# Recurrent branch of a hybrid step: another form of the decay root, gate products on VectorE, weights split one stage earlier and kept in DRAM

## The chip, the core and the metric

The kernel runs on one core of a Trainium2 chip. The metric is the device time in microseconds (us) of one launch. The engines of the core run side by side, each its own instructions in their written order: TensorE (PE, matrix products), VectorE (DVE), ScalarE (ACT), GpSimd (POOL) and SyncE (SP, which here issues most of the DMA transfers). An instruction starts when those ahead of it on its engine have started and the semaphores it waits for are set, so an instruction that waits holds up all that is written behind it on its engine.

## The reference, cut to what matters

One step of a two-layer backbone on 512 latent tokens and 128 context tokens, width 1024. The even layer has two branches, attention and a gated linear recurrence (RG-LRU) over 512 channels in both directions, and one output projection over both. The odd layer is differential attention. What the change touches is the recurrence:

```python
def rglru(x, w_a, b_a, w_x, b_x, lam, h0, reverse):
    ...
    r = jax.nn.sigmoid(jnp.einsum('btnc,ncd->btnd', xb, w_a).reshape(b, t, wd) + b_a)
    i = jax.nn.sigmoid(jnp.einsum('btnc,ncd->btnd', xb, w_x).reshape(b, t, wd) + b_x)
    log_a = -LRU_C * r * jax.nn.softplus(-lam)
    a = jnp.exp(log_a)
    u = jnp.sqrt(-jnp.expm1(2 * log_a)) * (i * x)
    ...
    a_acc, u_acc = lax.associative_scan(combine, (a, u), reverse=reverse, axis=1)
    hs = u_acc + a_acc * h0[:, None, :]
    final = hs[:, 0] if reverse else hs[:, -1]
    return hs, final

def even_layer_lat(...):
    ...
    o_a = neighbourhood_attention(q, k, v, ck, cv, rpb).reshape(b, t, NA_WIDTH)
    o_b, _, _ = lru_branch(xb, conv_w, conv_b, wa, ba, wx, bx, lam, lru_state[:, 0], lru_state[:, 1])
    o = jnp.concatenate([o_a * jax.nn.silu(ga), o_b * jax.nn.silu(gb)], axis=-1) @ w_out
    return x + gate * o
```

The combine step is h[t] = a[t]·h[t-1] + u[t]. `lru_branch` runs a depthwise convolution of width 4 and then `rglru` in both directions, and adds the two.

Products are done in three matmuls of a split operand (hi·hi + lo·hi + hi·lo), so every weight and every activation that goes into TensorE is first split into a rounded part `hi` and the rest `lo`.

## The kernel before, in words

One program runs in five stages, in each of which TensorE's work is a list of matmul groups (`fill`) and all the rest are `side` tasks. `run` merges the two: each group of the list has a cost, and a side task is written into the program when the sum of the costs reaches the task's position. The positions and lags stand in tables of numbers at the top of the file (`E1_POS`, `LRU_POS`, `LRU_LAG`, `XB_LAG`, `E3_POS` and so on). So the order of the instructions on each engine is fixed when the program is built.

The stages, with their times in the profiled execution:
- E0, to 75 us: conditioning and the V projection.
- E1, 75 to 218.5 us, the attention stage: 8 neighbourhood-attention heads, with the q, k and gate projections between them.
- E2, 218.5 to 330.4 us, the recurrent stage: the projections xb (input of the recurrence) and gb (its gate), the recurrence in 4 blocks of 128 channels (numbers 0 to 3 in the names, so xc3 is block 3), and the half "oa" of the output projection (attention part, `opea` in the names).
- E3, 330.4 to 386.6 us: the other half "eb" of the output projection (recurrent part, `op`), the residual, the norm of the odd layer (transposes `trx`), V of the odd layer.
- O, to 787.7 us: differential attention and the final norm.

A block of the recurrence: `xb_fill` copies the projection into `XB` (ACT), makes the convolution `xc` (one ACT and three DVE instructions, L791 to L793) and splits it into `xh` and `xl`. `lru_gate` makes the four gate products `g` on PE, with tanh on ACT into `thr` (decay gate) and `thi` (input gate), L814. `lru_a` makes `aa` = a (exp, L824) and tanh(L825) on ACT, (1+thi)·xc on DVE (L826), a² into `ss` on POOL (L828) and thr = (ss+1)·thr on DVE (L829), which is 1-a². `lru_b`, once for two blocks, takes the root on ACT (L835) and multiplies thi by it (L839: 6 of the 8 products on POOL, 2 on DVE). `lru_c` runs the four scans of a block on DVE (L846 to L853), copies the final states (`fin`) and adds both directions on POOL (L856). `lru_d` multiplies the sum into the gate path `oT` on DVE (L862, L864). `thr` and `thi` have two buffers each, so the first gate of block 2 waits until `lru_d` of block 0 has read its buffer.

Weights: a class keeps a list of loads. SP loads one of 512 KB into a staging tile (`_st`), ACT makes `hi` (L101), DVE makes `lo` by a subtraction (L102). The output weights of the even layer are four such loads for "oa" (`woea00` to `woea11`) and four for "eb" (`woeb00` to `woeb11`); the gate weights of the recurrence are four loads `lws` of 256 KB, split in E2 too.

## Time and profile before

| | us |
|---|---|
| median of 3 runs (790.59 to 790.83) | 790.82 |
| the profiled execution, its own time | 789.51 |
| its span, first to last instruction | 787.7 |
| PE busy, of the span | 738.8 (94%) |
| DVE busy | 566.7 (72%) |
| ACT busy | 401.0 (51%) |
| POOL busy | 276.9 (35%) |

The rows of the trace stand further down in numbered groups. Times in them are microseconds from the start of the span unless marked ns. In a timeline row the first number is the start, the second the duration, then engine, source line, operation, output and inputs, shape, and in brackets how long the engine stood idle before it and what released it. A row of waits gives the total, the count and the longest. A row of instructions by line gives the count and the durations in ns as minimum/median/maximum, or busy time and mean. Granted clock (PEclk) is TensorE's clock as a share of the full 2.4 GHz; its lower level is 1.2 GHz.

### The profile page before, as it was taken

The page shows a single profiled execution, that of the slowest core. Times are in us where ns is not written, and L with a number is a line of the kernel's source. Part 1 is how long each engine was busy: PE and PEld are TensorE (multiplying, and loading weights), DVE is VectorE, ACT ScalarE, POOL GpSimd, SP SyncE. Part 2 cuts the span into 40 slices and gives each one's busy share as a digit, 9 for nine tenths or more (in the row PEclk, how much of TensorE's full clock was granted, in tenths as well). Part 3 has the DMA queues.
Part 4 walks back from the last instruction along what each step waited for, and adds up shares of the span by engine and source line. Part 5 has one row for each costly group of instructions (what it writes and reads, how often), then busy time and mean ns, then how long its engine had stood idle before and what let it go on. Part 6 is the DMA issues. An engine that isn't in the chain of part 4 may idle for free.

```text
span 787.7 us, 13005 instructions
## 1 busy us (share of the span) xinstructions
PE 738.8 (94%) x4964; PEld 674.5 (86%) x4964; DVE 566.7 (72%) x1009; ACT 401.0 (51%) x836; POOL 276.9 (35%) x257
## 2 busy tenths in 40 slices
PE   4999999999999878799989999999999999999993
PEld 2679999989889866577989999999999999978872
DVE  3446677776656989868566678676878687887966
ACT  5355456555547675147444545545555555553423
POOL 3221211121001746443474164425544363212354
PEclk9999999999999989899999999999999999999997
DMA  8825433432381124395241122022211312241203
GB/s 343 319 72 188 171 112 114 141 125 101 111 303 65 51 84 134 109 378 188 96 146 47 64 88 74 22 89 66 68 44 47 117 55 78 64 139 49 91 1 133
DMA packets 33630, 92.32 MB, mean 117 GB/s; under 512 B 4272, under 2 KB 9200, under 8 KB 33568
## 3 DMA queue, kind: packets, MB, share of 16 engines
q1 hardware_dynamic: 31248, 88.10, 32.0%
q10 hardware_dynamic: 1920, 3.15, 1.7%
q8 instruction: 39, 0.64, 0.3%
q0 software_dynamic: 400, 0.25, 0.1%
q14 instruction: 23, 0.19, 0.1%
HBM read 79.94 MB, written 8.39 MB: 112 GB/s over the span
## 4 chain that ended last, share of the span: by engine, by line
PE 41%; DVE 9%; ACT 3%; issue 1%; POOL 1%; DMA 0%; ACTq 0%; DVEq 0%; POOLq 0%
PE ov L183 2%; PE ov L184 2%; PE ov L185 2%; PE dk L183 2%; PE dk L185 2%; PE dk L184 2%; PE opoa L185 2%; PE ds L1204 2%; PE opoa L183 2%; PE ds L1203 2%; PE dpt L1242 2%; PE opoa L184 2%; PE dq L183 2%; PE dq L185 2%; PE dq L184 2%; PE dg L183 1%
## 5 line engine op out<-in xcount | busy, mean ns | idle before, releaser
L1208 ACT ACTIVATE de<-ds,dnm 128x640 f32<-128x640 f32 x64 | 51.0, 796 | 105.6 <-DVE dnm L1206 105.6
L1206 DVE TENSOR_REDUCE dnm<-ds 128x1 f32<-128x640 f32 x64 | 52.3, 818 | 22.7 <-PE ds L1299 10.6
L569 POOL TENSOR_SCALAR_AFFINE_SELECT Tm<-rb 128x64 f32<-128x64 f32 (+1 forms) x24 | 8.8, 366 | 112.0 <-DMA rb<-in_rpb 93.2
L183 PE MATMUL ov<-owv_hi,hT_hi 128*128 128x256 f32 x160 | 46.5, 291 | 0.1
L184 PE MATMUL ov<-owv_lo,hT_hi 128*128 128x256 f32 x160 | 45.3, 283 | 0.0
L185 PE MATMUL ov<-owv_hi,hT_lo 128*128 128x256 f32 x160 | 45.2, 282 | 0.0
L183 PE MATMUL dk<-hT_hi,dk_hi 128*128 128x320 f32 x128 | 41.7, 326 | 0.0
L183 PE MATMUL dq<-hT_hi,dq_hi 128*128 128x320 f32 x128 | 41.0, 320 | 0.5 <-ACT vc L1092 0.5
L183 PE MATMUL dg<-hT_hi,dg_hi 128*128 128x320 f32 x128 | 41.0, 320 | 0.0
L1204 PE MATMUL ds<-dKL,dQ 128*128 128x320 f32 x128 | 38.9, 312 | 1.9 <-DVE dKL L487 1.9
L185 PE MATMUL dk<-hT_hi,dk_lo 128*128 128x320 f32 x128 | 40.3, 314 | 0.0
L184 PE MATMUL dk<-hT_lo,dk_hi 128*128 128x320 f32 x128 | 40.2, 314 | 0.0
L185 PE MATMUL dq<-hT_hi,dq_lo 128*128 128x320 f32 x128 | 39.6, 309 | 0.0
L185 PE MATMUL dg<-hT_hi,dg_lo 128*128 128x320 f32 x128 | 39.6, 309 | 0.0
L184 PE MATMUL dq<-hT_lo,dq_hi 128*128 128x320 f32 x128 | 39.6, 309 | 0.0
L184 PE MATMUL dg<-hT_lo,dg_hi 128*128 128x320 f32 x128 | 39.6, 309 | 0.0
L1203 PE MATMUL ds<-dKH,dQ 128*128 128x320 f32 x128 | 39.4, 316 | 0.1
L1230 DVE SCALAR_TENSOR_TENSOR de<-de,drs,de 128x640 f32<-128x640 f32 x32 | 35.8, 1120 | 1.1
L102 DVE TENSOR_TENSOR PTl<-pt,PTh 128x512 fp32r<-128x512 f32 x24 | 16.6, 692 | 26.0 <-ACT PTh L101 24.4
L102 POOL TENSOR_TENSOR dq_lo<-dq_st,dq_hi 128x1024 fp32r<-128x1024 f32 x8 | 21.4, 2678 | 29.9 <-ACT dq_hi L101 29.9
L183 PEld LDWEIGHTS ov<-owv_hi,hT_hi 128*128 128x128 f32 x160 | 30.3, 190 | 1.0 <-DVE sgdg L468 0.5
L102 DVE TENSOR_TENSOR dPTl<-dpt,dPTh 128x512 fp32r<-128x512 f32 (+1 forms) x48 | 28.5, 594 | 3.7 <-ACT dPTh L101 3.7
(481 smaller groups left out, 2788.2 us busy)
## 6 DMA issues: line engine op xcount, KB each, us to landing
aste<-in_e_ada_w SPq DMA_DIRECT2D x16, 512.0 KB, 5.7
asto<-in_o_ada_w SPq DMA_DIRECT2D x16, 512.0 KB, 5.5
astge<-in_e_ada_g SPq DMA_DIRECT2D x8, 512.0 KB, 6.1
owv_st<-in_o_wv SPq DMA_DIRECT2D x8, 512.0 KB, 3.3
astgo<-in_o_ada_g SPq DMA_DIRECT2D x8, 512.0 KB, 7.1
dq_st<-in_o_w SPq DMA_DIRECT2D x8, 512.0 KB, 3.3
dk_st<-in_o_w SPq DMA_DIRECT2D x8, 512.0 KB, 3.5
dg_st<-in_o_w SPq DMA_DIRECT2D x8, 512.0 KB, 3.3
```

What stands on the lines that cost most here:

```text
L102: after(lag, lambda: (eng.tensor_tensor(lo, src, hi.bitcast(F32), ALU.subtract), done and done()))
L183: PE.matmul(out, ah, bh, start=start, stop=False)
L184: PE.matmul(out, ah, bl, start=False, stop=False)
L185: PE.matmul(out, al, bh, start=False, stop=stop)
L569: G.affine_select(dst, src, pattern=[[8, n], [0, 8]], compare_op=ALU.is_ge, fill=NEG, base=8 * jj + 7, channel_multiplier=-1)
L1203: PE.matmul(sp[:, b, 0:HALF], qs, KH[:, a, ks], start=True, stop=False)
L1204: PE.matmul(sp[:, b, 0:HALF], qs, KL[:, a, ks], start=False, stop=True)
L1206: V.tensor_reduce(nm[:, a : a + 1], sp[:, :, 0:HALF], AX.XY, ALU.max, negate=True)
L1208: S.activation(e, sp[:, :, 0:HALF], AF.Exp, bias=nm[:, a : a + 1], accum_out=rs[:, a : a + 1])
L1230: V.scalar_tensor_tensor(e0_, e0_, rs[:, 0:1], e1_, ALU.mult, ALU.add)
L1242: PE.transpose(tp[:, 256 * m + 128 * c : 256 * m + 128 * c + 128], p[:, 128 * kt : 128 * kt + 128], ident)
```

## The change

- The root. sqrt(1-a²) is made as (1+a)·sqrt(tanh(...)), with half the argument in the tanh. The square on POOL is gone, and so is its tile. The root is taken of `thr` straight after the tanh, and one DVE instruction for each block, thr = (aa+1)·thr, stands behind the root instead of ahead of it.
- All 8 gate products are on DVE. The sum of both directions stays on POOL for blocks 0 to 2 and is on DVE for block 3; it goes into `thi`.
- `thr` and `thi` have three buffers.
- Ten splits are made in E1: for each, SP loads 512 KB into `est`, ACT casts `hi` into a part of `oT` that is not used yet, DVE subtracts in place, and SP stores both parts to DRAM. Two carry the gate weights, eight the output weights. In E2 and E3 their `hi` and `lo` come from DRAM by two loads in place of one, with no work on ACT or DVE.
- The tables of positions for E2, E3 and the early splits have other numbers. The O stage's step is the same 13.0 under another name.

The core of the diff:

```diff
-            lambda: V.tensor_scalar_mul(cn, u3, 4.0),
+            lambda: V.tensor_scalar_mul(cn, u3, 2.0),
...
-            woea.append([W.add(I["e_wo"][i, q], [128, 2, 512], f"woea{i}{q}") for q in range(2)])
+            woea.append([W.late(f"woea{i}{q}", [128, 2, 512]) for q in range(2)])
...
+                if src is None:
+                    need(("early", name))
+                    for dst, x in zip((hi, lo), self.parts[name]):
+                        SP.dma_start(dst[:].bitcast(F32), x)
+                    put("w", self.done)
...
+    ehis = [oT[:, k : k + 2].rearrange("p a b -> p (a b)")[:, 0:1024].bitcast(F32R) for k in (4, 6)]
+    def early_split(n, p):
...
+        def load():
+            st["w"] = ep.tile([128, 1024], F32, tag="est", name=f"est{n}", bufs=EARLY_BUFS)
+            SP.dma_start(st["w"], src if len(shape) == 4 else src.rearrange("p a b -> p (a b)"))
+        def low():
+            V.tensor_tensor(st["w"][:].bitcast(F32R), st["w"], ehi.bitcast(F32), ALU.subtract)
+        def store():
+            put("early", name)
+            SP.dma_start(flat[0], ehi.bitcast(F32))
+            SP.dma_start(flat[1], st["w"])
+        return [(p - EARLY_LAG[0], load), (p, lambda: S.copy(ehi, st["w"])), (p + EARLY_LAG[1], low), (p + EARLY_LAG[2], store)]
...
-            st["thr"] = lp.tile([128, 2, XL], F32, tag="thr", name=f"thr{i}", bufs=2)
-            st["thi"] = lp.tile([128, 2, XL], F32, tag="thi", name=f"thi{i}", bufs=2)
+            st["thr"] = lp.tile([128, 2, XL], F32, tag="thr", name=f"thr{i}", bufs=3)
+            st["thi"] = lp.tile([128, 2, XL], F32, tag="thi", name=f"thi{i}", bufs=3)
...
-        for d in range(2):
-            G.tensor_tensor(ss[:, d], aa[:, d], aa[:, d], ALU.mult)
-        after(LRU_LAG[0], lambda: (V.scalar_tensor_tensor(thr, ss, 1.0, thr, ALU.add, ALU.mult), put("la", i)))
+        put("la", i)
...
-            thr, thi = lru_st[j]["thr"], lru_st[j]["thi"]
+            thr, thi, aa = lru_st[j]["thr"], lru_st[j]["thi"], lru_st[j]["aa"]
+            V.scalar_tensor_tensor(thr, aa, 1.0, thr, ALU.add, ALU.mult)
             for d in range(2):
-                (V if ((1, 0), (0, 0), (1, 0), (0, 0))[j][d] else G).tensor_tensor(thi[:, d], thi[:, d], thr[:, d], ALU.mult)
+                (G if LRU_POOL[j][d] else V).tensor_tensor(thi[:, d], thi[:, d], thr[:, d], ALU.mult)
...
-        G.tensor_tensor(hs[:, 0], hs[:, 0], hs[:, 1], ALU.add)
+        (G if LRU_POOL[i][2] else V).tensor_tensor(u[:, 0], hs[:, 0], hs[:, 1], ALU.add)
...
-    hooks = {(0, 0): lambda: W.split(wob[1][0], E3_LAG[3]), (0, 2): lambda: W.split(wob[1][1], E3_LAG[4]),
+    hooks = {(0, 2): lambda: W.split(wob[1][1], E3_LAG[4]),
```

How the instructions stand now, at three places. First VectorE in the recurrent stage, around the convolution of the fourth block, xc3 (the last number in a name only tells tiles apart). Before, from the second gate of the third block on:

```order
L468 SCALAR_TENSOR_TENSOR oT_127<-sgtgb21_3267,gb2_1_3233 128x320
L839 TENSOR_TENSOR thi0_2994<-thi0_2994,thr0_2993 128x644
L846 SCALAR_TENSOR_TENSOR thr0_2993<-aa0_3076,lru_s_269,thi0_2994 128x512
L847 SCALAR_TENSOR_TENSOR thr0_2993<-aa0_3076,thi0_2994 128x128
L852 SCALAR_TENSOR_TENSOR thr0_2993<-aa0_3076,lru_s_269,thi0_2994 128x512
L853 SCALAR_TENSOR_TENSOR thr0_2993<-aa0_3076,thi0_2994 128x128
L102 TENSOR_TENSOR woea00_lo_3313<-woea00_st_3105,woea00_hi_3312 128x1024
L793 SCALAR_TENSOR_TENSOR xc3_3346<-XB1_2830,conv_265,xc3_3346 128x644 x3
L862 SCALAR_TENSOR_TENSOR oT_127<-thr0_2993,oT_127 128x8x64
L864 SCALAR_TENSOR_TENSOR oT_127<-thr0_2993,oT_127 128x128
```

And now, from the same gate on:

```order
L489 SCALAR_TENSOR_TENSOR oT_127<-sgtgb21_3333,gb2_1_3297 128x320
L846 SCALAR_TENSOR_TENSOR xc3_3393<-XB1_2910,conv_265,xc3_3393 128x644 x3
L891 SCALAR_TENSOR_TENSOR thr0_3107<-aa0_3301,thr0_3107 128x1288
L893 TENSOR_TENSOR thi0_3108<-thi0_3108,thr0_3107 128x644 x2
L891 SCALAR_TENSOR_TENSOR thr1_3196<-aa1_3272,thr1_3196 128x1288
L893 TENSOR_TENSOR thi1_3197<-thi1_3197,thr1_3196 128x644 x2
L107 TENSOR_TENSOR xl3_3399<-xc3_3393,xh3_3398 128x644
L489 SCALAR_TENSOR_TENSOR oT_127<-sgtgb30_3435,gb3_0_3400 128x320
L900 SCALAR_TENSOR_TENSOR thr0_3107<-aa0_3301,lru_s_269,thi0_3108 128x512
L901 SCALAR_TENSOR_TENSOR thr0_3107<-aa0_3301,thi0_3108 128x128
```

The convolution xc3 stood behind the scans of block 0 and a weight split and stands ahead of them now; the roots and products of blocks 0 and 1 stand between it and its split xl3.

Second, SyncE's queue at the end of the recurrent stage, from the last "oa" weight to the first loads of E3 (`xae` and `spill` are the residual's tiles and their way to DRAM, `xr` is the residual's load in E3). Before:

```order
L120 DMA woea11_st_3427<-in_e_wo 128x1024
L962 DMA xaexa_3464<-in_xs 128x512 x2
L962 DMA xaegbias_3465<-in_xp 128x512
L120 DMA woeb00_st_3501<-in_e_wo 128x1024
L969 DMA spill2_67<-xaexa_3464 128x512 x2
L969 DMA spill2_67<-xaegbias_3465 128x512
L962 DMA xaegbias_3465<-in_xs 128x512
L962 DMA xaexa_3464<-in_xs 128x512
L120 DMA woeb01_st_3631<-in_e_wo 128x1024
L962 DMA xaexa_3464<-in_xp 128x512
L120 DMA woeb10_st_3658<-in_e_wo 128x1024
```

Now:

```order
L149 DMA woea11_hi_3669<-woea11_h_703 128x1024
L149 DMA woea11_lo_3670<-woea11_l_704 128x1024
L1023 DMA spill2_67<-xaegbias_3512 128x512
L1016 DMA xaexa_3511<-in_xp 128x512
L149 DMA woeb00_hi_3696<-woeb00_h_705 128x1024
L149 DMA woeb00_lo_3697<-woeb00_l_706 128x1024
L1023 DMA spill2_67<-xaegbias_3512 128x512
L1023 DMA spill2_67<-xaexa_3511 128x512
L149 DMA woeb01_hi_3779<-woeb01_h_707 128x1024
L149 DMA woeb01_lo_3780<-woeb01_l_708 128x1024
L1023 DMA spill2_67<-xaexa_3511 128x512
L1057 DMA out_lru<-fin_118 128x8
```

Each output weight is two loads straight into the tiles that TensorE reads, and woea11 now stands behind seven of the residual's transfers that it stood ahead of (they are above this piece). The load of woeb10 follows behind out_lru, the store of the final states.

Third, VectorE in the attention stage, in the third of its four parts. Before:

```order
L606 RECIPROCAL rs23_1537<-rs23_1537 128x1
L607 TENSOR_SCALAR P23_1535<-P23_1535,rs23_1537 128x384
L508 TENSOR_REDUCE cnme1_1565<-cs10_1563 128x1
L508 TENSOR_REDUCE cnme1_1565<-cs11_1564 128x1
L300 TENSOR_SCALAR MTo_108<-adaTo2_1577,o_ada_bT_259 128x2
L301 TENSOR_SCALAR MTo_108<-adaTo2_1577,o_ada_bT_259,o_normT_261 128x2
L102 TENSOR_TENSOR PTl20_1591<-pt20_1585,PTh20_1590 128x512
```

Now:

```order
L627 RECIPROCAL rs23_1577<-rs23_1577 128x1
L628 TENSOR_SCALAR P23_1575<-P23_1575,rs23_1577 128x384
L770 TENSOR_TENSOR est3_1387<-est3_1387,oT_127 128x1024
L529 TENSOR_REDUCE cnme1_1611<-cs10_1609 128x1
L529 TENSOR_REDUCE cnme1_1611<-cs11_1610 128x1
L321 TENSOR_SCALAR MTo_108<-adaTo2_1623,o_ada_bT_259 128x2
L322 TENSOR_SCALAR MTo_108<-adaTo2_1623,o_ada_bT_259,o_normT_261 128x2
L107 TENSOR_TENSOR PTl20_1637<-pt20_1631,PTh20_1636 128x512
```

The subtraction of the fourth early split (est3) is a new row ahead of the softmax work of the next heads; the other nine stand in the same way at other places of the stage.

## Rows read from the trace of the kernel before

**Rows 1.** Windows by stage: E1, then E2; the first line names the columns.
```profile
core 0: us, PE busy (x) PEld busy (x) DVE busy (x) ACT busy (x) POOL busy (x), PEclk, DMA share, GB/s
75.00:218.50 143.50, 142.96 (x1102) 132.85 (x1101) 97.67 (x264) 77.67 (x186) 19.85 (x65) 1.00 0.37 127
218.50:330.40 111.90, 95.77 (x546) 84.11 (x544) 92.61 (x95) 65.36 (x88) 49.15 (x33) 0.95 0.35 121
```
**Rows 2.** Waits of PE, whole run: total us, times, longest.
```profile
PE g L183 <- ACT thr L814: 7.1, 1, 7.1
...
PE op L183 <- ACT oh L101: 2.4, 1, 2.4
PE op L185 <- DVE ol L102: 2.2, 1, 2.2
...
PE opea L184 <- DVE woea_lo L102: 1.9, 1, 1.9
...
PE opea L183 <- ACT woea_hi L101: 1.6, 1, 1.6
PE trx L1066 <- DVE xo L1056: 1.2, 1, 1.2
```
**Rows 3.** Timeline of PE: the matmuls that end its longest and its last E2 wait.
```profile
280.42 0.64 PE L183 MATMUL g<-xh,lwh 128*128 128x322 f32 x1 [7.10 <-ACT thr L814]
...
330.42 0.80 PE L185 MATMUL op<-woeb_hi,ol 128*128 128x512 f32 x1 [2.22 <-DVE ol L102]
```
**Rows 4.** Timeline of ACT in the same stretch as the long wait.
```profile
277.01 0.73 ACT L101 CAST xh<-xc 128x644 fp32r<-128x644 f32 x1 [8.64 <-DVE xc L793]
278.27 1.28 ACT L814 ACT_TABLE_LOAD   x1 [0.53 <-DVE oT L864]
```
**Rows 5.** Timeline of DVE, ops with and without POOL beside them.
```profile
252.47 2.74 DVE L793 SCALAR_TENSOR_TENSOR xc<-XB,conv,xc 128x644 f32<-128x644 f32 x3 [1.52 <-ACT xc L791]
...
260.53 1.50 DVE L829 SCALAR_TENSOR_TENSOR thr<-ss,thr 128x1288 f32<-128x1288 f32 x1
...
265.14 2.49 DVE L846 TENSOR_TENSOR_SCAN thr<-aa,lru_s,thi 128x512 f32<-128x512 f32 x1
...
273.09 3.89 DVE L793 SCALAR_TENSOR_TENSOR xc<-XB,conv,xc 128x644 f32<-128x644 f32 x3
276.89 1.08 DVE L862 SCALAR_TENSOR_TENSOR oT<-thr,oT 128x512 f32<-128x512 f32 x1
...
278.09 1.28 DVE L846 TENSOR_TENSOR_SCAN thr<-aa,lru_s,thi 128x512 f32<-128x512 f32 x1
...
281.09 0.81 DVE L102 TENSOR_TENSOR xl<-xc,xh 128x644 fp32r<-128x644 f32 x1
```
**Rows 6.** Instructions of three lines, E2: ns minimum/median/maximum, first and last start.
```profile
L826 DVE SCALAR_TENSOR_TENSOR thi<-thi,xc x8: 821/1356/1891, 243.2 to 300.6; 128x644 f32<-128x644 f32 x8
L828 POOL TENSOR_TENSOR ss<-aa x8: 1678/1827/1845, 243.4 to 301.9; 128x644 f32<-128x644 f32 x8
L856 POOL TENSOR_TENSOR thr<-thr x4: 1556/1582/2197, 273.2 to 323.0; 128x644 f32<-128x644 f32 x4
```
**Rows 7.** DVE by line and shape, 218 to 331: busy us, mean ns, idle before.
```profile
L102 DVE TENSOR_TENSOR woea_lo<-woea_st,woea_hi 128x1024 fp32r<-128x1024 f32 x4 | 7.1, 1774 | 0.7 <-ACT woea_hi L101 0.7
...
L102 DVE TENSOR_TENSOR woeb_lo<-woeb_st,woeb_hi 128x1024 fp32r<-128x1024 f32 x3 | 3.6, 1211 | 0.0
...
L102 DVE TENSOR_TENSOR lwl<-lws,lwh 128x512 fp32r<-128x512 f32 x4 | 2.7, 686 | 1.3 <-ACT lwh L101 1.3
```
**Rows 8.** ACT by line and shape in E1: a cast of 1024 columns.
```profile
L101 ACT CAST k_hi<-k_st 128x1024 fp32r<-128x1024 f32 x3 | 3.2, 1052 | 0.0
```
**Rows 9.** Waits of DVE in E1: total us, times, longest.
```profile
DVE PTl L102 <- ACT PTh L101: 24.4, 23, 2.0
```
**Rows 10.** DMA issues 215 to 345: count, KB each, median us to landing.
```profile
woea_st<-in_e_wo SPq DMA_DIRECT2D x4, 512.0 KB, 3.5
```
**Rows 11.** Windows of 10 us: the start of E3.
```profile
330.00:340.00 10.00, 9.58 (x31) 7.70 (x32) 4.62 (x6) 1.05 (x1) 2.68 (x2) 0.72 0.89 288
```

More of the change, by code (lines that the diff above doesn't have):

```diff
@@ L34 @@
 LAG_E1 = (2.13, 0.0)
-LAG_E2 = (0.2, 3.75)
-LAG_E3 = (3.85, 1.06)
+LAG_E2 = (0.0, 4.36)
+LAG_E3 = (4.55, 1.39)
 LAG_O = (1.0, 0.98)
@@ L62 @@
 HOLD = 2
+EARLY_LAG = (8.46, 0.92, 1.0)
+EARLY_POS = ((5.4, 8.46, 16.0), (3.43, 13.56, 16.4), (3.0, 14.38, 12.44), (2.99,))
+EARLY_BUFS = 2
+LRU_POOL = ((0, 0, 1), (0, 0, 1), (0, 0, 1), (0, 0, 0))
 KORD = (0, 2, 4, 6, 1, 3, 5, 7)
@@ L114, in add, with late @@
             return len(self.todo) - 1
+        def late(self, name, shape, pool=None, bufs=None):
+            return self.add(None, shape, name, pool, bufs)
         def load(self, n):
@@ L133, in split @@
                     lo = pool.tile(list(shape), F32R, tag="wlo", name=name + "_lo", bufs=bufs)
+                if src is None:
+                    need(("early", name))
+                    for dst, x in zip((hi, lo), self.parts[name]):
+                        SP.dma_start(dst[:].bitcast(F32), x)
+                    put("w", self.done)
+                    self.ready[self.done] = (hi, lo)
+                    self.done += 1
+                    self.load(self.done + 1)
+                    continue
                 st = self.staged.pop(self.done)
@@ L408, in body @@
         if kind == "oa":
-            woa.append([W.add(I["e_wo"][i, q], [128, 2, 512], f"woea{i}{q}") for q in range(2)])
+            woa.append([W.late(f"woea{i}{q}", [128, 2, 512]) for q in range(2)])
         else:
             wid[f"{kind}{i}"] = wcol("e_w", (12 if kind == "xb" else 16) + i, f"{kind}{i}")
-    wob = [[W.add(I["e_wo"][half, 2 + q], [128, 2, 512], f"woeb{half}{q}", *(("op", 2) if half else ())) for q in range(2)] for half in range(2)]
+    wob = [[W.late(f"woeb{half}{q}", [128, 2, 512], *(("op", 2) if half else ())) for q in range(2)] for half in range(2)]
     W.hold = wob[1][0]
@@ L729, in gb_fill @@
         return proj_silu(ep if i < 2 else lp, wid[f"gb{i}"], f"gb{i}", lambda sg: None, oT[:, 4 + i])
+    early = [(I["lru_w"][2 * n : 2 * n + 2].rearrange("i p g n -> p i g n"), [128, 2, 4, 128], f"lw{n}") for n in range(2)]
+    early += [(I["e_wo"][i, 2 * x + q], [128, 2, 512], f"woe{'ab'[x]}{i}{q}") for x in range(2) for i in range(2) for q in range(2)]
+    ehis = [oT[:, k : k + 2].rearrange("p a b -> p (a b)")[:, 0:1024].bitcast(F32R) for k in (4, 6)]
+    def early_split(n, p):
+        src, shape, name = early[n]
+        ehi = ehis[n % 2]
+        W.parts[name] = [dram.tile(shape, F32, tag=f"{name}_{x}", name=f"{name}_{x}") for x in "hl"]
+        flat = [p.rearrange("p a b c -> p (a b c)" if len(shape) == 4 else "p a b -> p (a b)") for p in W.parts[name]]
+        st = {}
+        def load():
[8 more added lines that the diff above has]
+        return [(p - EARLY_LAG[0], load), (p, lambda: S.copy(ehi, st["w"])), (p + EARLY_LAG[1], low), (p + EARLY_LAG[2], store)]
     fill = q_fill(0) + k_fill(0)
@@ L734, in body @@
     now = sum(c for c, _ in fill)
+    n_early = 0
     for i in range(4):
@@ L747, in body @@
         side += na_ctx(i, start + E1_POS[i][2])
+        for p in EARLY_POS[i]:
+            side += early_split(n_early, start + p)
+            n_early += 1
         if i < 3:
@@ L773, in lru_w @@
     def lru_w(i):
-        st = lp.tile([128, 4, 128], F32, tag="lws", name=f"lws{i}")
-        SP.dma_start(st, I["lru_w"][i])
+        need(("early", f"lw{i // 2}"))
         hi = lp.tile([128, 4, 128], F32R, tag="lwh", name=f"lwh{i}", bufs=2)
@@ L778, in lru_w @@
         lw[i] = (hi, lo)
-        return lambda: (split(hi[:], lo[:], st[:]), put("lw", i))
+        for dst, x in zip((hi, lo), W.parts[f"lw{i // 2}"]):
+            SP.dma_start(dst[:].bitcast(F32), x[:, i % 2])
+        put("lw", i)
     def xb_fill(i):
@@ L815, in lru_gate @@
                      bias=lb[:, 4 * i + g : 4 * i + g + 1])
+        put("g", i)
     def lru_a(i):
+        need(("g", i), n=4)
         st = lru_st[i]
@@ L820, in lru_a @@
         st["aa"] = aa = lp.tile([128, 2, XL], F32, tag="aa", name=f"aa{i}", bufs=2)
-        st["ss"] = ss = lp.tile([128, 2, XL], F32, tag="ss", name=f"ss{i}")
         for d in range(2):
@@ L1023, in body @@
     W.pools["op"], W.hold = op, None
+    W.split(wob[1][0])
     wvo = {0: [W.add(I["o_wv"][0, q], [128, 4, 256], f"owv0{q}") for q in range(2)]}
```

30 lines of the change are left out of this document (16 added, 14 removed).

## The prediction
> **What bounds the kernel now.** I read the windows by stage first [rows 1]. In E1 TensorE is busy 142.96 of 143.50 us: nothing there can be won, it can only be lost. In E2 it is busy 95.77 of 111.90, and VectorE 92.61, more than any other helper. So E2 is the stage to look at, and 111.90 - 95.77 = 16.1 us of idle PE are what an edit in it can give back. The granted clock of 0.95 means that a tenth of the time ran at the lower level, about 0.05 x 111.9 = 5.6 us lost; PE's own work in E2 is therefore 95.77 - 5.6 = 90.2 us, and PE alone could be done with E2 at 218.5 + 90.2 = 308.7. No gain from E2 can be over 21.7 us.
>
> Next the waits of PE over the whole run [rows 2]. One takes 7.1 us, the first gate of block 2; then come four of 1.6 to 2.4 on splits of output weights and of the recurrent output. I followed the long one back. The gate matmul needs its `xh` and a free `thr`. `xh` starts at 277.01 after 8.64 us in which ACT waited for xc [rows 4], so ACT was ready at 268.37. xc started on DVE only at 273.09 and took 3.89 [rows 5], because scans of block 0 and a weight split stood ahead of it. The tanh then waits for `lru_d` of block 0, the last reader of the buffer [rows 4]. The matmul restarts at 280.42 [rows 3]. The last wait of E2 ends at 330.42 [rows 3], on `ol`, the end of a DVE chain of scans, lru_d and splits. Behind it the first 10 us of E3 have clock 0.72 [rows 11]. So E2 is bound by the in-order DVE, first at xc3, then at ol.
>
> **The price of POOL beside DVE.** The same DVE instruction is longer when a POOL instruction on SBUF runs beside it: L826 takes 821 ns at least and 1891 at most [rows 6], a scan 1.28 or 2.49, the convolution 2.74 or 3.89 [rows 5]. That is +1.07, +1.21, +1.15; I take 1.1 us for each overlap.
>
> **Removed.** From DVE in E2 and the first rows of E3: four woea_lo (7.1), three woeb_lo (3.6), four lwl (2.7), in sum 13.4 us [rows 7], inflation of two woea_lo included. From ACT about as many casts; ACT has room, so they count for nothing by themselves, but two waits of PE (woea_hi 1.6, woea_lo 1.9) [rows 2] lose their cause. From POOL: eight squares of 1.83 and six products. Their overlaps with DVE go with them.
>
> **Added to DVE.** Six of the eight products at 0.82 (L826's undisturbed 821, same width): +4.9. The root instruction, 1.5 as L829 undisturbed [rows 5], takes the place of L829, so 0. One sum of directions: +0.8. Net on DVE in E2: 13.4 - 5.7 = 7.7 less, before contention.
>
> **Moved: the walk along DVE.** Nothing ahead of xc3 sits in PE's way, before or now, so PE comes to xb3 at the same time and ACT hands over xc at 268.37 as above. By the order, DVE has nothing but two splits and the pair for block 0 ahead of that and is free: xc3 starts at 268.4 instead of 273.09. From there I add what stands on DVE up to the first ol: xc3 2.74; four roots of 1.5; eight products, four thi, one sum and xl3, 14 of 0.82; four scan sets at 3.0 (278.09 to 281.09 [rows 5]); four lru_d at 1.2 (276.89 to 278.09); 5 splits of ooa, 6 gated products, 2 residual sums, one ol, 14 of 0.69 (512 columns, as lwl); two gate products of some 0.5. Sum 2.7 + 6.0 + 11.5 + 12.0 + 4.8 + 9.7 + 1.0 = 47.7. Rows that follow each other overlap a little (273.09 + 3.89 = 276.98 against a next start of 276.89 [rows 5]); with 0.05 for each of some 30 that I did not take start to start it is 1.5: 46.2. Start 268.4 + 46.2 = 314.6. Six POOL instructions still run beside it (sums of directions for blocks 0 to 2, three or so residual sums): + 6 x 1.1 = 6.6. Waits that I see left (the sum of block 2 on POOL, the cast of oh): 1.3. The first ol is then ready, and E3 in full course, at 322.5 instead of 330.42: **7.9 us gained.** Since DVE is never free on this way, PE's shorter waits don't add to it. They are: first gate of block 2 some 2.2 us, still behind two table loads, two roots and a cast on ACT (three buffers spare it the lru_d); ooa some 3.7, now behind roots, products and scans; woea11 1.1, its loads wait for the tile's last reader (3.0 us of matmuls against 3.5 from issue to landing [rows 10]); end of E2 4.8, much as now.
>
> **Early splits in E1.** Ten times a cast of 1.05 on ACT [rows 8] and a subtraction of 1.21 on DVE [rows 7] go into in-order queues beside a PE that never waits. In this stage DVE waits 24.4 us in 23 times for the probabilities' cast [rows 9], about 1.06 each, so there is idle time near most of the splits. The bound below is 0. The bound above is the whole 22.6 us on PE's way, if each stands in a chain that PE waits for; the trace shows idle ahead of the consumers, so I take 0.7 (one split of ten in full view of a wait with little slack, a third of 2.27) and keep 0 to 4.
>
> **E3.** The loads of woeb10 and woeb11 stand on SP behind out_lru, which waits for POOL's last final states, and hi and lo are 1 MB in a stretch where DMA engines are 0.89 busy [rows 11]: 0 to 2 us. The transposes come some 0.5 earlier in the fill, so their present wait of 1.2 [rows 2] grows by about 0.7. I take 1.0 together, range 0 to 3. O is the same: 0.
>
> **Sum.** 7.9 - 0.7 - 1.0 = 6.2. The profiled execution of 789.51 becomes 783.3; the median of 790.82, 1.3 above it, becomes **784.6**.
>
> **The rivals.**
> B, contention nearly gone. If the remaining POOL instructions fall into places where DVE reads PSUM or waits, the walk ends at 316 to 318.8, the gain is 11.6 to 14 with part of the low clock avoided, and after 0.7 to 1.7 of cost the time is 777 to 780. For it: POOL had 49.15 us in E2 [rows 1] and loses over half. Against: the six left lie just on the part where DVE is never idle.
>
> C, DVE stands still for the whole of each POOL instruction, and loads come late. A convolution started within 0.1 us of a POOL sum that took 2.20 (median 1.58 [rows 6]) and lost 1.15 [rows 5], so the trace shows less than a whole stop. If it were whole, six overlaps would cost up to 1.58 each, 9.5 in place of 6.6, E3 would start at 325.4, and 5.0 less 1.7 for E1 and E3 leaves 787.5; with woea11 and woeb11 up to 1 us late each, up to 789.5.
> By the Trainium skill, SBUF — State Buffer, section "SBUF: two separate sides", the port that VectorE and GpSimd share is a lock held for a whole instruction, and the loser blocks. The sum by that rule alone would be 787.5 where mine is 784.6, and the trace agrees with it only in part, with its 1.15 of 1.58.
>
> S, no difference: E2 ends on a latency chain from cast to subtraction to sum that the moved work doesn't shorten, and the early splits eat the rest: 789.3 to 792.3. For it: the end-of-E2 wait is about as long by my walk as now.
>
> D, slower: the early splits stand in chains. Each adds 1.05 on ACT and 1.21 on DVE, 2.26 in series for whatever is written behind it, the cast and the split of the probabilities above all, where the idle time is some 1.06 each [rows 9]. If PE's chain has no more slack than that, a split costs 2.26 - 1.06 = 1.2; with two of the ten away from the probabilities that is 9.6, and 7.9 - 9.6 - 1.0 = -2.7 gives 793.5. It decides from 0.7 us per split, where the gain is gone. For it: PE busy without a gap says only that work comes in time, not with how much to spare. Against it: DVE is busy 97.67 of 143.50 and ACT 77.67 [rows 1], so what a split delays can catch up before the next one, some 14 us later.
>
> **How the numbers follow.** A .52, B .16, C .14, S .10, D .08. The likeliest is A: 784.6, its own range 782 to 787. For 8 in 10 I leave out the lower part of B (.08), D (.08) and what of S is above 790 (.05): 779 to 790. About 0.2%, 1.6 us, is what a measurement of this kernel can tell from no change. Faster by more than that: A, B and C, .82; within it, S, .10; slower, D, .08.
>
> **What would show it right or wrong.** Right: xc3 starts on DVE near 268.4, PE's wait for the first gate of block 2 falls from 7.1 to some 2, DVE runs without a gap from there to ol, the POOL instructions beside it cost about 1.1 each, the first ol ends near 322, E1 ends within 1 us of 218.5. Wrong in E1: new waits of PE on DVE or ACT there, and each later stage late by as much. Wrong in the walk: gaps on DVE ahead of a scan or a root, which would mean that ACT's roots and table loads, not DVE, set the pace. Wrong in E3: PE waiting for woeb10 or woeb11 from DMA.

## The result

The changed kernel takes 782.17 us (median of 4 runs, 780.81 to 783.55) against 790.71 of the kernel before beside it: ratio 0.9901, interval 0.9884 to 0.9918. The forecast was 784.6. Beside some of the experiments it was measured once more with 782.77 against 790.62, ratio 0.9898. The profiled execution took 782.90 by its own time (span 781.1), 6.6 less than the 789.51 of before. The medians differ by 8.5, since before's profile lies 1.2 below the 790.71 and this one 0.7 above its median; so the traces account for 6.6 of the 8.5.

To see where, I cut the PE timeline of every kernel at the same matmuls: E1 from the first V projection to the first xb, E2 from there to the third group of the "eb" half, E3a to the eighth of its second item, E3b until the odd layer's key projections are under way, O1 through the odd layer's first scores, and the rest. All are differences of start times of one profiled execution.

| kernel | time ratio to before | E1 | E2 | E3a | O1 |
|---|---|---|---|---|---|
| before | 1 | 199.6 | 114.5 | 17.7 | 71.3 |
| changed | 0.9901 | 200.5 | 109.5 | 17.7 | 69.7 |
| changed, again | 0.9898 | 199.9 | 109.1 | 18.7 | 69.8 |

The two stretches left out (E3b with 18.9 us up to V and 26.1 or 25.3 behind it; the rest of O with 308.8 to 309.1) differ by 0.8 and 0.3. So E2 gained 5.0, E3b 0.8 and O1 1.6, and E1 lost 0.9; another 0.4 was lost ahead of E1.

The windows by stage of the changed kernel, with the columns of [rows 1]:

```profile
75.00:219.50 144.50, 143.60 (x1101) 132.72 (x1100) 110.21 (x276) 85.67 (x195) 26.07 (x64) 1.00 0.70 235
219.50:326.00 106.50, 95.59 (x547) 83.59 (x546) 74.58 (x91) 56.59 (x77) 19.99 (x18) 0.97 0.46 164
```

VectorE's busy time in E2 fell from 92.61 to 74.58 and GpSimd's from 49.15 to 19.99; PE's idle time there only from 16.1 to 10.9. The waits of PE from the first xb on, which answer [rows 2]:

```profile
PE op L204 <- ACT oh L106: 3.5, 1, 3.5
PE opea L206 <- DVE ooa L107: 2.3, 1, 2.3
PE g L204 <- ACT thr L867: 1.9, 1, 1.9
PE trx L1121 <- DVE xo L1111: 1.8, 1, 1.8
PE opea L204 <- DMA woea_hi<-woea_h: 1.3, 1, 1.3
PE opea L204 <- ACT ooa L106: 1.0, 1, 1.0
PE opea L205 <- DMA woea_lo<-woea_l: 0.8, 1, 0.8
```

The wait of 7.1 for the first gate of block 2 is 1.9 now, the two on weight splits (1.9 and 1.6) are gone, and of the two at the end of E2 (2.4 and 2.2) one of 3.5 is left. Two new kinds stand in their place: for ooa on VectorE (that on ACT, 1.0, was there before), and for the DMA of woea11. The timeline of VectorE, at the places that answer [rows 5]:

```profile
269.81 2.74 DVE L846 SCALAR_TENSOR_TENSOR xc<-XB,conv,xc 128x644 f32<-128x644 f32 x3 [2.04 <-ACT xc L844]
272.46 1.50 DVE L891 SCALAR_TENSOR_TENSOR thr<-aa,thr 128x1288 f32<-128x1288 f32 x1
...
283.01 3.15 DVE L107 TENSOR_TENSOR ooa<-oT,ooa 128x512 fp32r<-128x512 f32 x3
...
290.87 2.58 DVE L880 SCALAR_TENSOR_TENSOR thi<-thi,xc 128x644 f32<-128x644 f32 x2
...
295.90 0.69 DVE L953 TENSOR_TENSOR optmpae<-opea,gate_e 128x512 f32<-128x512 f32 x1 [0.60 <-PE opea L206]
...
302.86 2.55 DVE L893 TENSOR_TENSOR thi<-thi,thr 128x644 f32<-128x644 f32 x2
...
310.19 0.69 DVE L953 TENSOR_TENSOR optmpae<-opea,gate_e 128x512 f32<-128x512 f32 x1 [1.76 <-PE opea L206]
...
316.87 0.69 DVE L953 TENSOR_TENSOR optmpae<-opea,gate_e 128x512 f32<-128x512 f32 x1 [1.68 <-PE opea L206]
...
319.10 2.31 DVE L900 TENSOR_TENSOR_SCAN thr<-aa,lru_s,thi 128x512 f32<-128x512 f32 x1
...
325.94 1.29 DVE L107 TENSOR_TENSOR ol<-oT,oh 128x512 fp32r<-128x512 f32 x2 [0.54 <-ACT oh L106]
```

The convolution xc3 starts as soon as ACT hands it over and has its undisturbed 2.74 instead of 3.89. The first ol starts at 325.94. On the way there are four rows lengthened by GpSimd (3.15, 2.58, 2.55, 2.31) and, unlike the forecast, three that wait for PE (0.60, 1.76, 1.68).

### The profile page after: what moved, and what is told of

The parts are those of the page before. It is cut to its first block, busy times and chain, and to the rows that moved or that the text cites. A ratio compares the mean times of both kernels' runs of the same rounds, so it can differ in the third digit from the quotient of the medians.

```text
span 781.1 us, 13085 instructions
## 1 busy us (share of the span) xinstructions
PE 735.6 (94%) x4964; PEld 670.1 (86%) x4964; DVE 559.7 (72%) x1014; ACT 399.4 (51%) x834; POOL 252.9 (32%) x242
## 3 DMA queue, kind: packets, MB, share of 16 engines
q10 hardware_dynamic: 1920, 3.15, 1.6%
## 4 chain that ended last, share of the span: by engine, by line
PE 39%; DVE 10%; ACT 3%; issue 1%; POOL 1%; DMA 0%; ACTq 0%; DVEq 0%; POOLq 0%
PE ov L204 2%; PE ov L205 2%; PE ov L206 2%; PE dpt L1297 2%; PE opoa L204 2%; PE opoa L205 2%; PE ds L1259 2%; PE opoa L206 2%; PE ds L1258 2%; PE dq L204 2%; PE dq L206 2%; PE dq L205 2%; PE dk L204 2%; PE dk L206 2%; PE dk L205 2%
## 5 line engine op out<-in xcount | busy, mean ns | idle before, releaser
L1261 DVE TENSOR_REDUCE dnm<-ds 128x1 f32<-128x640 f32 x64 | 52.1, 817 | 19.9 <-PE ds L1354 10.9
L590 POOL TENSOR_SCALAR_AFFINE_SELECT Tm<-rb 128x64 f32<-128x64 f32 (+1 forms) x24 | 12.1, 503 | 109.7 <-DMA rb<-in_rpb 109.7
L106 ACT CAST dPTh<-dpt 128x512 fp32r<-128x512 f32 (+1 forms) x48 | 24.8, 517 | 11.3 <-PE dpt L1297 11.3
```

The costliest lines, as they stand in the source:

```text
L106: S.copy(hi, src)
L590: G.affine_select(dst, src, pattern=[[8, n], [0, 8]], compare_op=ALU.is_ge, fill=NEG, base=8 * jj + 7, channel_multiplier=-1)
L1261: V.tensor_reduce(nm[:, a : a + 1], sp[:, :, 0:HALF], AX.XY, ALU.max, negate=True)
```

## The experiments

The table above goes on with the experiments; each is told below.

| kernel | time ratio to before (95%) | E1 | E2 | E3a | O1 |
|---|---|---|---|---|---|
| early_alone | 1.0001 (0.9982 to 1.0020) | 200.9 | 115.5 | 16.7 | 69.8 |
| order_thr3 | 1.0015 (1.0002 to 1.0029) | 199.9 | 115.7 | 17.2 | 71.1 |
| root_only | 1.0047 (1.0033 to 1.0062) | 200.1 | 119.7 | 16.8 | 69.8 |
| weights_only | 1.0033 (1.0021 to 1.0046) | 200.0 | 115.6 | 20.0 | 69.8 |
| weights_lags | 0.9989 (0.9976 to 1.0003) | 200.0 | 109.7 | 22.7 | 69.8 |
| weights_order | 0.9981 (0.9962 to 0.9999) | 203.7 | 109.8 | 21.7 | 69.8 |
| no_early | 1.0089 (1.0058 to 1.0119) | 199.8 | 121.3 | 20.0 | 71.2 |
| pool_products | 0.9950 (0.9930 to 0.9969) | 200.3 | 109.9 | 19.1 | 69.7 |
| scan3_4 | 0.9905 (0.9891 to 0.9919) | 199.4 | 108.0 | 18.4 | 71.2 |
| sums_dve | 0.9904 (0.9884 to 0.9923) | 199.8 | 106.8 | 18.4 | 71.2 |
| sums_score | 0.9912 (0.9895 to 0.9929) | 203.8 | 108.3 | 18.3 | 69.1 |

**The early splits alone (early_alone).** To the kernel before:

```diff
+        for p in EARLY_POS[i]:
+            side += early_split(n_early, start + p)
+            n_early += 1
```

> The kernel before, with the ten early splits of the change added to the attention stage (loads, casts, subtractions, stores) and nothing else; their results are not used. My theory: they cost what the attention stage ended later in the changed kernel, 219.55 against 218.23, less 0.15 that was there from the start of the trace: 1.2 us, so 791.9 (791.3 to 792.6). Rival D: each costs up to 0.96 us: 800. Rival: they cost nothing and the 1.2 us is chance: 790.7.

Measured: 790.09 against 790.49, ratio 1.0001. The splits cost at most the 0.2% that the interval leaves. Rival D, a cost of up to 9.6 us, has fallen. My 1.2 is inside the interval, and so is nothing at all. In the profiles the kernels without early splits have E1 from 199.6 to 200.1, most of those with them 199.4 to 200.9. Two profiles stand out with 203.7 and 203.8, to which the last section comes back.

**The change without the early splits (no_early).** To the changed kernel:

```diff
-EARLY_POS = ((5.4, 8.46, 16.0), (3.43, 13.56, 16.4), (3.0, 14.38, 12.44), (2.99,))
+EARLY_POS = ((), (), (), ())
...
-            woea.append([W.late(f"woea{i}{q}", [128, 2, 512]) for q in range(2)])
+            woea.append([W.add(I["e_wo"][i, q], [128, 2, 512], f"woea{i}{q}") for q in range(2)])
```

and the same for the eb and the gate weights.

> The changed kernel without the early splits: gate and output weights are loaded and split in the recurrent stage and E3 as before; root, products on VectorE, three buffers and positions stay. My theory (VectorE bounds E2, and what counts is its work there): E1 ends 1.2 us earlier, and 4 x 0.69 + 7 x 1.21 = 11.2 us of subtractions come back on VectorE, of which up to 5 us go into its waits: E2 ends 6 to 11 later, in sum 787 to 792. Rival: root, order and buffers bring the gain and the splits cost only their 1.2: 781 to 783.

Measured: 796.79, ratio 1.0089; 14 us slower than the change and 6 slower than before. The rival (781 to 783) has fallen: without the splits nothing of the gain is left. My range ended at 792, so the size was off too. Part of it is that the positions of the change suit the loads of the change: ACT waited 11.8 us in all for the loads of the gate weights, and the first late tanh (PE waits 2.1 at 246.31) already costs before xc3. So the 14 us are more than the splits are worth within the change, by an amount that no run gives.

**Order and third buffer alone (order_thr3).** To the kernel before:

```diff
-            after(LRU_LAG[1 + j - i + 1], lambda j=j: lru_c(j))
+            after(LRU_LAG[1 + j - i + 1] + (XL0 if j == 0 else 0.0), lambda j=j: lru_c(j))
...
-            st["thr"] = lp.tile([128, 2, XL], F32, tag="thr", name=f"thr{i}", bufs=2)
+            st["thr"] = lp.tile([128, 2, XL], F32, tag="thr", name=f"thr{i}", bufs=3)
```

with XL0 = 1.8.

> The kernel before, with the scans of block 0 behind the convolution of block 3 instead of ahead of it, and three buffers for thr. Both theories: PE's wait of 7.1 us for the first gate of block 2 falls to 2 to 3. My theory (VectorE is the bound, so PE's wait comes back later): ratio 0.998 to 1.000, 789.2 to 790.7. Rival (a wait is worth its length): 4 to 5 us less, 786.

Measured: 791.70, ratio 1.0015, if anything slower: 1 us above my range, and the rival's 786 has fallen. The waits of PE:

```profile
PE opea L184 <- ACT ooa L102: 4.6, 1, 4.6
PE g L184 <- ACT thr L815: 2.8, 1, 2.8
PE op L184 <- ACT oh L102: 2.5, 1, 2.5
PE op L186 <- DVE ol L103: 1.9, 1, 1.9
```

The longest wait fell from 7.1 to 2.8 as both said, and a new one of 4.6 for ooa stands right behind it: the scans that were moved back are ahead of it on VectorE now. A wait removed from PE is worth nothing while the queue that feeds it has as much to do.

**The root alone (root_only).** To the kernel before:

```diff
-        for d in range(2):
-            G.tensor_tensor(ss[:, d], aa[:, d], aa[:, d], ALU.mult)
-        after(LRU_LAG[0], lambda: (V.scalar_tensor_tensor(thr, ss, 1.0, thr, ALU.add, ALU.mult), put("la", i)))
+        put("la", i)
...
+            V.scalar_tensor_tensor(thr, aa, 1.0, thr, ALU.add, ALU.mult)
```

> The kernel before with the new form of the root alone: no squares on GpSimd, the root straight after the tanh, one VectorE instruction behind it. My theory: VectorE's (1+thi)xc lose their overlaps, on the path four of them at 1.07 at most, 2.1 by the mean of 1.36 against 0.82, and 1.1 of one L829; the way from exp to the products is shorter by the 3.6 us of two squares, but the wait for the first gate of block 2 is untouched: 787 to 789.5. Rival: the instruction now stands between root and products, on the chain itself, and takes back what the squares gave: 790 to 792.

Measured: 794.18, ratio 1.0047: slower than both ranges. The wait for the first gate of block 2 grew from 7.1 to 10.1: the two root instructions stand on VectorE between the roots on ACT and xc3, one of them lengthened:

```profile
265.34 1.50 DVE L835 SCALAR_TENSOR_TENSOR thr<-aa,thr 128x1288 f32<-128x1288 f32 x1 [1.23 <-ACT thr L832]
266.87 0.83 DVE L837 TENSOR_TENSOR thi<-thi,thr 128x644 f32<-128x644 f32 x1
267.62 2.88 DVE L835 SCALAR_TENSOR_TENSOR thr<-aa,thr 128x1288 f32<-128x1288 f32 x1
...
277.15 3.89 DVE L793 SCALAR_TENSOR_TENSOR xc<-XB,conv,xc 128x644 f32<-128x644 f32 x3
```

xc3 starts at 277.15 in place of 273.09. So the new root does harm in the old order; that the new order alone would make it harmless was not tried.

**The weights alone (weights_only), and with the positions of the loads (weights_lags).** The first is the kernel before with early splits, `late` loads and the new `lru_w`; the second has besides:

```diff
-LAG_E2 = (0.2, 3.75)
-LAG_E3 = (3.85, 1.06)
+LAG_E2 = (0.0, 4.36)
+LAG_E3 = (4.55, 1.39)
...
-E2_LAG = (0.84, 0.95)
+E2_LAG = (2.04, 5.04)
```

and E3_LAG and the place of woeb10 as in the change.

> The kernel before with the weight part of the change alone: ten early splits in the attention stage, hi and lo from DRAM in the recurrent stage and E3; root, products, buffers and positions as before. My theory (VectorE's work in the recurrent stage is the bound): 13.4 us less on VectorE there, of which xc3 gets 1.9 (one lwl, one woea_lo) and the stretch from xc3 to the first ol the rest less its waits, 6 to 9 us in sum: 781 to 785. Rival (it takes the new order, the third buffer and the products too): the wait of 7.1 us stays near 6 and the time is 787 to 790.

> The kernel before with the weight part and the positions of the weight loads and the residual's transfers from the change (LAG_E2, LAG_E3, E2_LAG, E3_LAG, woeb10 at the start of E3); root, products, buffers and the recurrence's positions as before. With the weight part alone the loads of woea11 and woeb01 stood on SP behind stores that waited for GpSimd, and PE waited 5.5 and 4.3 us for them. Theory now: with these loads in time PE's end of E2 is set by the first ol, which was ready near 327.6 there: 787 to 789.5; the wait of some 6 us for the first gate of block 2 stays. Rival: the loads were not the cause, and it stays at 792.8.

Measured: 792.82 (ratio 1.0033) and 789.01 (0.9989). My theory, that VectorE's work in E2 is the bound, gave 781 to 785 for the first and has fallen in this form: with 13 us less to do on VectorE the kernel was slower, above the rival's 787 to 790 too. The second lies in its 787 to 789.5. The loads show why. SP's queue in weights_only, ahead of woea11:

```profile
304.73 0.32 SPq L1020 DMA_DIRECT2D spill<-xaegbias  x1
305.10 0.42 SPq L1013 DMA_DIRECT2D xaegbias<-in_xs  x1
305.62 0.40 SPq L1013 DMA_DIRECT2D xaexa<-in_xs  x1
306.11 0.38 SPq L147 DMA_DIRECT2D woea_hi<-woea_h  x1
```

In the changed kernel the same load leaves at 302.89:

```profile
302.89 0.32 SPq L149 DMA_DIRECT2D woea_hi<-woea_h  x1
```

In weights_only the store ahead of it waits for an addition on GpSimd that ends at 304.71, and all loads behind wait with it; PE waited 5.5 us for woea11 and 4.3 for woeb01. With the load positions of the change (weights_lags) E2 is 109.7, as short as in the change with 109.5, though root, products and xc3's order are the old ones and the wait of 5.6 for the first gate is still there. The gain is then lost in E3a, 22.7 instead of 17.7, and the waits there are again on loads (2.4, and 0.8 of the 1.3):

```profile
PE op L202 <- DMA woeb_hi<-woeb_h: 2.4, 1, 2.4
PE op L203 <- DMA woeb_lo<-woeb_l: 1.3, 2, 0.8
```

Only 1.9 of the 5.0 is more idle time of PE. The rest is its clock: the same 71 matmuls are busy 18.77 us at a granted clock of 0.85, and 15.66 at 0.99 in the changed kernel. The windows of E3a, of before, of the changed kernel and of weights_lags (columns as in [rows 1]):

```profile
332.72:350.42 17.70, 16.51 (x71) 13.39 (x70) 9.08 (x13) 5.88 (x10) 7.69 (x7) 0.92 0.98 355
```

```profile
329.04:346.74 17.70, 15.66 (x71) 12.46 (x70) 8.56 (x12) 5.52 (x11) 7.94 (x7) 0.99 1.02 407
```

```profile
328.42:351.12 22.70, 18.77 (x71) 14.54 (x72) 8.01 (x12) 4.88 (x9) 7.29 (x7) 0.85 0.98 389
```

That the waits on loads brought the clock down is likely, since matmuls behind them take 0.6 to 0.8 us instead of 0.39, but no run held one without the other.

SP's queue in weights_lags, against the same place in the changed kernel:

```profile
326.31 0.32 SPq L1020 DMA_DIRECT2D spill<-xaexa  x1
326.68 0.42 SPq L1054 DMA_DIRECT2D out_lru<-fin  x1
327.20 0.41 SPq L147 DMA_DIRECT2D woeb_hi<-woeb_h  x1
```

```profile
321.95 0.38 SPq L1023 DMA_DIRECT2D spill<-xaexa  x1
324.15 0.34 SPq L1057 DMA_DIRECT2D out_lru<-fin  x1
324.58 0.38 SPq L149 DMA_DIRECT2D woeb_hi<-woeb_h  x1
```

The first "eb" matmul of PE, here and then in the changed kernel:

```profile
324.48 0.50 PE L202 MATMUL op<-woeb_hi,oh 128*128 128x512 f32 x1 [3.13 <-ACT oh L104]
```

```profile
325.96 0.72 PE L204 MATMUL op<-woeb_hi,oh 128*128 128x512 f32 x1 [3.53 <-ACT oh L106]
```

The load of woeb10 leaves 2.7 behind it here and 1.4 ahead of it there. The last store of the residual, behind which it stands, waits for GpSimd's last residual addition, which ends at 326.28 here and at 320.3 there (there the load waits for out_lru, whose last final states GpSimd has copied at 324.13). That addition waits for the last gated product on VectorE. This is at 316.87 in the changed kernel (rows above), ahead of the scans of block 3, and here behind the sum on GpSimd and what multiplies it into oT:

```profile
321.60 2.12 DVE L913 SCALAR_TENSOR_TENSOR oT<-thr,oT 128x512 f32<-128x512 f32 x1 [1.01 <-POOL thr L907]
323.64 0.27 DVE L915 SCALAR_TENSOR_TENSOR oT<-thr,oT 128x128 f32<-128x128 f32 x1
323.85 0.67 DVE L950 TENSOR_TENSOR optmpae<-opea,gate_e 128x512 f32<-128x512 f32 x1
```

So what the rest of the change brings over splits and load positions is not a shorter E2 but an end of E2 in which the residual is done early and the loads for E3 leave in time. Whether the root, the products, the buffers or the recurrence's positions do that, these two runs don't separate; the next but one says that the products don't need to be on VectorE for most of it.

**The weights, the load positions and the order (weights_order).** To weights_lags: the two edits of order_thr3.

> As the weight part with the load positions, and besides the scans of block 0 behind the convolution of block 3 and three buffers for thr. Theory: order alone gave nothing (1.0015) because VectorE was full behind xc3; with the splits off VectorE the same order has room: 783.5 to 786.5. Rival: the new root and the products on VectorE are needed too, and it stays within 1 us of the kernel without the order.

Measured: 788.77, ratio 0.9981. My 783.5 to 786.5 has fallen; it stays within 1 us of weights_lags, as the rival said: the first gate waits 1.3 in place of 5.6, ooa 6.0 in place of 1.0, E2 is 109.8 against 109.7. Both experiments on the order agree.

**The products on GpSimd (pool_products).** To the changed kernel:

```diff
-LRU_POOL = ((0, 0, 1), (0, 0, 1), (0, 0, 1), (0, 0, 0))
+LRU_POOL = ((0, 1, 1), (1, 1, 1), (0, 1, 1), (1, 1, 0))
```

> The changed kernel with six of the eight gate products on GpSimd again, as before the change; all else stays. My theory: VectorE has 6 x 0.82 = 4.9 us less of its own and up to six overlaps at 1.05 more, 6.3, so +1.4 (0 to +3): 783.5 (782 to 785). Rival C (VectorE stands still for the whole of each GpSimd instruction of 1.7): 10.2 - 4.9 = +5.3: 787.5.

Measured: 784.92, ratio 0.9950. By the medians that is some 2.4 slower than the change, near my 783.5 and in its range; by the ratios it is 3.9, and their interval reaches 787.5, the time of rival C. So the time alone doesn't settle C; its price is settled by the rows. E2 loses 0.4 and E3a 1.4 against the first profile of the change, 0.8 and 0.4 against the second. E3a is 19.1 and not the 22.7 of weights_lags, though six products are on GpSimd in both, so most of that is carried by the rest: root, third buffer for `thi`, the sum of block 3 on VectorE and the recurrence's positions, which no run separates. The root instruction of block 1 has a product beside it now:

```profile
273.88 2.18 POOL L893 TENSOR_TENSOR thi<-thi,thr 128x644 f32<-128x644 f32 x1 [51.62 <-DVE thr L891]
274.57 2.84 DVE L891 SCALAR_TENSOR_TENSOR thr<-aa,thr 128x1288 f32<-128x1288 f32 x1
```

against 1.49 without: +1.35, where 1.49 of the GpSimd row (273.88 to 276.06) was left when it started.

**The sums on VectorE (sums_dve).** To the changed kernel: the last entry of each row of LRU_POOL is 0.

> The changed kernel with all four sums of directions on VectorE. By the overlaps in its trace: two sums on GpSimd lengthen VectorE's instructions by 1.08 and 1.02, the third lies beside waits; on VectorE each costs 0.83: -2.1 + 2.5 = +0.4, so 782 to 784. By whole stops of 1.57 each it would be -3.1 + 2.5 = -0.6: 781.5 to 782.5; the two are hardly to be told apart by the time, but by the rows.

Measured: 783.02, ratio 0.9904: the same time within the intervals, as expected, but the rows say more. E2 is 106.8, 2.3 to 2.7 shorter than in the two profiles of the change, where I had +0.4. The three ooa splits lie without a sum beside them and take 1.89 in place of 3.15:

```profile
283.50 1.89 DVE L107 TENSOR_TENSOR ooa<-oT,ooa 128x512 fp32r<-128x512 f32 x3
```

PE waits 0.4 for ooa instead of 2.3, and VectorE's waits for PE further on all but go: 1.5 us idle from xc3 to ol against 5.9. O1 gives back 1.5, which is the granted clock again (last section), and E3a 0.7 against the first profile of the change and nothing against the second.

**The scans of block 3 one place earlier (scan3_4).** To the changed kernel:

```diff
-            after(LRU_LAG[1 + j - i + 1], lambda j=j: lru_c(j))
+            after(4.0 if j == 3 else LRU_LAG[1 + j - i + 1], lambda j=j: lru_c(j))
```

> The changed kernel with the scans of block 3 and their sum one place earlier on VectorE, ahead of the last gated product of the output half and of the sum of block 2 into oT. In the changed kernel's trace VectorE waits there 1.68 us for PE with the scans behind it. My theory: the first ol is ready 1.7 to 2.7 earlier: 780.5 against 782.2 of the changed kernel. Rival: the gated product comes 3.5 us later, PE waits for its PSUM buffer, and nothing is gained: 782.

Measured: 783.16 against 782.77 of the changed kernel beside it: no gain in the time, so my 780.5 has fallen, and the 782 of the rival is nearer. Its reason isn't seen, since PE waits for no PSUM buffer there. E2 is 108.0, 1.1 to 1.5 shorter, so the move does what it says; E3a is longer by 0.7 or shorter by 0.3 than in the two profiles of the change, and O1 is 1.4 longer.

**The changed kernel once more (after_again).**

> The changed kernel once more, beside the others on one chip: 782.2 (780.8 to 783.6) as measured first. The spread of some 3 us between executions is expected to go with stretches at the lower granted clock that come or not.

Measured: 782.77 (781.45 to 783.85). In this profile E2 and O1 are the same as in the first within 0.4, E1 is 0.6 shorter and E3a 1.0 longer. The spread of 2.4 us is as wide as that of any experiment's difference here, so the small ones are read from stages, not from times. That the clock makes the spread, as expected, is not shown by these two, which both have 69.7 to 69.8 in O1.

**A score later (sums_score).** To sums_dve:

```diff
-side += [(p + x, lambda h=h, t=2 * pp + n // 2, a=n % 2: score(h, t, a)) for n, x in enumerate(OD_SCORE)]
+side += [(p + x + (1.86 if k + n == 0 else 0.0), lambda h=h, t=2 * pp + n // 2, a=n % 2: score(h, t, a)) for n, x in enumerate(OD_SCORE)]
```

> The changed kernel with all sums on VectorE, and in the odd layer the first score of the first head 1.86 cost units later in TensorE's list, behind key projections that need nothing new. In all traces PE waits there 1.7 to 1.9 us for the low part of the keys, and in those of before, of the scans moved and of the sums on VectorE the granted clock falls right behind it, which costs some 1.5 more. Theory: the wait goes, and with it the low clock behind it: 1.8 to 3.3 less than the 783.0 of the kernel with the sums alone: 780 (779.5 to 781.5). Rival: the softmax chain behind the first score is as late as before and PE waits the same 1.9 a few us on: 783.

Measured: 782.90, ratio 0.9912: nothing gained that can be measured; my 779.5 to 781.5 has fallen. (The profiled execution took 786.14, with a late copy in E1 that the last section tells of, as in weights_order.) The wait of 1.9 is gone and O1 is 69.1, but that is only 0.6 less than the 69.7 of the changed kernel, which had the wait and the same clock; three small waits of 0.2 to 0.3 for the softmax chain stand in its place, and what took the rest was not followed. No version here beats the changed kernel beyond the intervals.

## Why the prediction held, and where not

- **E1, 0.7 forecast.** The profile shows 0.9, the experiment with the splits alone nothing that can be measured. So 0.7 isn't contradicted, and neither is 0. D has fallen: 9.6 is far outside the interval.
- **Start of the walk.** xc3 was put at 268.4 with E1's delay apart; it started at 269.81, and E1 ended 1.32 later (219.55 against 218.23): 268.5. Right.
- **PE's shorter waits.** Gate 2.2 forecast, 1.85 seen; ooa 3.7, seen 1.0 + 2.3; woea11 1.1, seen 1.3 + 0.8; end of E2 4.8, seen 3.5. The kinds were right (the 1.0 of ooa was there before the change), woea11 too small by half.
- **The walk along VectorE is the step that was off.** Forecast to the end of the first ol: 46.2 of its own, 6.6 for overlaps, 1.3 of waits, 54.1 in sum. Seen from xc3 to the start of ol: 56.13, of which 50.22 busy and 5.9 idle; with the 0.69 of ol 56.8, so 2.7 longer. The price of an overlap was right, their number too high: of seven GpSimd instructions on the way four lengthen a row, by 1.26, 1.02, 0.98 and 1.03 against the same rows undisturbed, 4.3 in sum and not 6.6. What is left, 45.9, is the 46.2 less ol. The sentence "DVE is never free on this way, so PE's shorter waits don't add to it" was wrong: VectorE waits three times for PE, 4.0 us together, because its gated products stand in line behind matmuls that were held up by ooa and by woea11. The other idle time is 1.0 for the cast of ooa on ACT, 0.5 for that of oh, and small gaps. The two queues wait for each other by turns. So E2 brought 5.0 and not 7.9.
- **E3, -1.0 forecast.** The waits came nearly as forecast: the transposes wait 0.6 longer (1.82), loads of woeb cost 0.2 (0.8 in the second profile), and PE is idle 0.85 longer in E3a. Yet E3a is 17.7 as before, since its granted clock is 0.99 and was 0.92 before, and the same 71 matmuls are busy 0.85 less (windows under weights_lags). Behind E3a 0.8 came back, 0.5 of it a wait of PE for `vc`, a tile of the odd layer's V, that is gone. The loads were nearly in time because the residual was done early, which weights_lags shows by its opposite.
- **O, 0 forecast.** 1.6 came in O1 from the granted clock (1.00 against 0.98; the same 492 matmuls are busy 67.60 and 69.23), which is not the change's doing (last section).
- **The sum.** -0.7 + 7.9 - 1.0 = 6.2 against -0.9 + 5.0 + 0.8 + 1.6 + 0.3 - 0.4 = 6.4 by the parts, 6.6 by the own times and 8.5 by the medians. That it came out near is in part luck: the walk gave 2.9 too much, and the clock in O1 and in E3a made up for most of it. Without the 1.6 of O1 the parts give 4.8. Why the medians show 1.9 more than the profiles, no trace here tells.
- **The rivals.** B (contention nearly gone) fell: the walk ended at 325.94 and not by 318.8, and the time is not 777 to 780. In part its reason holds: with the sums off GpSimd E2 has 2.3 to 2.7 less, most of it as waits that vanish, but the time is the same. C's 787.5 fell, and its price of up to 1.58: an overlap costs 0.94 to 1.38 here, and less where little of the GpSimd row is left. Its figure for E2, 5.0 gained, is the one measured, but by VectorE's waits and not by overlaps. Its mechanism was nearer than the prediction took it, for VectorE loses nearly all that is left of the GpSimd row when it starts: 1.35 of 1.49 in pool_products. By the Trainium skill, SBUF — State Buffer, section "SBUF: two separate sides", the shared port is held for a whole instruction and the loser blocks; the rows agree, with 0.1 to 0.2 us less than the rest of the GpSimd row. S and D fell.
- **What was not asked in the prediction:** whether each part has a worth of its own. None that was tried has. Alone, splits with loads, order, and root each give ratios of 1.0015 to 1.0047, splits with loads at their new positions 0.9989; together 0.990. The products on VectorE and the recurrence's positions were not tried alone, and no run parts the root from those positions. VectorE's queue, the end of the residual and SP's queue are bounds that lie within a few us of each other, and what is taken off one shows only when the next is moved too.

## What to carry to other kernels

Work taken off a full in-order engine paid here only where the DMA queue that now feeds PE instead ran free: look at what each load stands behind, and whether a store ahead of it waits for a slow engine. Test a change of several parts by undoing one at a time, not only by doing one alone: here each part that was tried alone says "worthless", and the whole gains 1%. And a wait that vanishes is counted only after asking what the same queue has to do next: 7.1 us became 2.8 + 4.6 without a tenth of a percent of gain.
